# One layer of a diffusion backbone on one core: another order of the seven products of the FFNs' second matmul, later modulation vectors, and the final norm piece by piece

## The chip, the cores and the metric

The kernel runs on one core of a Trainium2 chip. The metric is the device time of one execution in microseconds; the median of the runs of one kernel is compared with the median of another's on the same chip.

## What is computed

One layer over 1024 latent tokens (width 1024) with 256 context tokens as a prefix: a half-step SwiGLU FFN, a mixer (short convolution beside attention, merged by gates), a second half-step FFN, and a final RMS norm. Each part is normed first and modulated by shift, scale and gate, nine vectors (`ml[0]` to `ml[8]`) that come from a small matmul of SiLU(c) with `w_mod`. Context tokens go through the first FFN and the mixer's projections only.

```python
def swiglu(h, w_in, w_out):
    a, b = jnp.split(h @ w_in, 2, axis=-1)
    return (jax.nn.silu(a) * b) @ w_out
...
        mod_lat = (jax.nn.silu(c) @ w_mod[layer] + b_mod[layer])[:, None, :]
...
        x = x + 0.5 * ml[2] * swiglu(modulate(rms_norm(x, norm1_g[layer]), ml[0], ml[1]),
                                      ffn1_w_in[layer], ffn1_w_out[layer])
...
        x = x + ml[5] * merge_branches(y_conv_l, o_l, gt_l, w_branch_conv[layer],
                                       w_branch_attn[layer], w_out[layer])
...
        x = x + 0.5 * ml[8] * swiglu(modulate(rms_norm(x, norm3_g[layer]), ml[6], ml[7]),
                                      ffn2_w_in[layer], ffn2_w_out[layer])
    return rms_norm(x, final_g)
```

## The kernel before

All matmuls are made of three: each 32-bit operand is split into a high part (a cast, on ACT) and a low part (a subtraction, on DVE), and high x high, high x low and low x high are added in PSUM. Left parts of weights are called `wl` and `wh` (two names, four buffers each, either holds both halves), right parts `rh`, `rl` or `r`.

Large products are taken as 2x2 blocks with seven block products instead of eight. The class `Winograd` does this for the products with columns of weights (the first matmul of both FFNs and the mixer), `row_products` for the FFNs' second matmul. There the right side is the hidden rows `hid` (22 rows of 128, upper and lower 11, left and right half: blocks b11, b12, b21, b22), written to DRAM as `hd` by the first matmul and fetched again. The left side is `w_out`, whose combinations are either loaded raw (products 1, 2, 4; two raw loads and a subtraction for product 7) or built in `ws` tiles by loads that add into them (`plus`, issued on GpSimd's queue; products 5, 6, 3). One product goes over 11 elements in 6 groups of two; each element is 12 matmuls, for 4 column tiles. Products 1, 6 and 7 add into one chain of four PSUM tiles (two of `pt`, one `po`, one `ps`), which is read out by adds into the latents `x` after each; the others use `ps` tiles. The hidden blocks are combined in place between products (`hid<-hid,hid` on DVE).

The stages, by time in the profiled execution: first FFN's first products until 720 us; its row products until 946, with the context's part of that FFN put in between in the last third of the first products; product 3's end and the norm that opens the mixer, until 972; the mixer until 1350; attention heads and merge until 2150; the second FFN's first products (the object `fast`) until about 2550; its row products until 2712; then product 3 of the second FFN, in two halves of 256 columns with its split operands held (`kept`), with the final norm beside it, until the end at 2768. In the second half `kept` is used again, one column tile after the other, each followed by its add into `x`.

The norm's scale for 512 columns comes as: squares (`sq`, ACT), sums by matmuls with a vector of ones into `pt`, an inverse square root on DVE (`rs_a`, `rs_y`), transposes with `ident` that spread it over partitions, and a multiplication of `x` by it, after which the shifted `x` is split into `r`. The final norm instead multiplies by a gain (`yf`), transposes `yf` into PSUM and scales the result on its way out (`ot`).

Modulation vectors 2 to 8 are made beside the first FFN's products: for each, `later_mod` loads rows of `w_mod` (`rawm`) and multiplies and adds them on DVE (`macc`), casts the sum on ACT (`acch`, `accl`), and finishes it with small matmuls, a copy and small stores and adds. It is a generator, of which a loop takes some steps a turn: `STEPS` in the first FFN, 11 in the mixer, and what is left at the mixer's end.

A scheduler places the instructions: each engine executes its list in order, and the order of the lists comes from a timeline made when the kernel is built, except for instructions that are pinned to program order. A step that waits therefore holds up everything behind it in its engine's list. SP's list issues most loads; its queue is a ring of eight.

The changed code in the kernel before:

Of the kernel before, what the change touches and what calls it, by code (L numbers as in the profile page):

```python
# [13 lines left out]
ALU = mybir.AluOpType  # L14
# [27 lines left out]
STEPS = (0, 6, 6, 6, 7, 7, 8, 8, 8, 15)  # L42
# [7 lines left out]
def tile_dit_layer(  # L50
# [413 lines left out]
    class Winograd:  # L464
# [6 lines left out]
        def __init__(self, xs, gain, mod, m, pairs, plain=False, ahead=3, side_from=None):  # L471
# [10 lines left out]
            self.n_squares = 0  # L482
# [18 lines left out]
        def norm0(self, in_place=False):  # L501

            acc = sum_squares(self.xs, C0)
            yield
            y = rstd_cols([acc], 512, D)
# [10 lines left out]
        def square(self, d):  # L516

            if not self.n_squares:
                self.acc = [ttile("sq_acc")]
            sq = ttile("sq") if self.n_squares else self.acc[0]  # L520
            act.activation(out=sq, in_=self.xs(d, C1), func=AF.Square)
            if self.n_squares == KD - 1:
                self.acc.append(sq)
            elif self.n_squares:
                dve.tensor_add(out=self.acc[0], in0=self.acc[0], in1=sq)
            self.n_squares += 1

        def norm1(self):
            y = rstd_cols(self.acc, 512, D)
# [215 lines left out]
    class Rows:  # L745


        def __init__(self, n, name):

            self.n, self.t = n, {}  # L750
# [15 lines left out]
        def fetch(self, src):  # L766

            for lower, c in ((0, 0), (0, 1), (1, 0), (1, 1)):
                for k, m in self.groups:
                    j = lower * self.n + k  # L770
                    load(self.t[k, lower, c], src[j : j + m, :, c * 512 : (c + 1) * 512].rearrange("a p n -> p a n"))

    def row_products(w, rows, add, after=lambda i, k: None, halves=False):
# [9 lines left out]

        R, groups = P * rows.n, rows.groups
        sums = {}
# [12 lines left out]

        def minus(t):
            act.activation(out=t, in_=t, func=AF.Copy, scale=-1.0)  # L800
# [13 lines left out]

        def operands(i, k, m):

            b11, b12, b21, b22 = (rows.t[k, v, c] for v in range(2) for c in range(2))
# [46 lines left out]
        for i in (1, 2, 4, 5, 6, 7) + (() if halves else (3,)):  # L864
            ps = chain if i in (1, 6, 7) else [ps_s() for _ in range(4)]
            for k, m in groups:
# [123 lines left out]
    half1.acc = accs  # L990
# [39 lines left out]
    def all_later_mods():  # L1030
# [5 lines left out]
        for m in range(2, 9):  # L1036
            yield from later_mod(m)

    steps = all_later_mods()


# [68 lines left out]

    gate1 = half_gate("gate1", 2)
# [22 lines left out]
    hs = Rows(NH // 2, "hid")  # L1134
    hs.fetch(hd)
# [570 lines left out]
```

## Time and profile before

| what | value |
|---|---|
| median of 3 runs | 2775.6 us (2775.3 to 2777.56) |
| profiled execution, own time | 2770.1 us |
| its span | 2768.2 us |
| granted TensorE clock, mean | 0.981 |
| PE (TensorE) busy | 96% |
| DVE (VectorE) busy | 73% |
| ACT (ScalarE) busy | 42% |
| POOL (GpSimd) busy | 20% |
| data moved | 354.37 MB, 128 GB/s on average |

A helper issues every instruction, so nearly all of them carry one line, 88, and the tile names tell them apart: `pt<-rh,wl` is a matmul into PSUM tile `pt` with those operands. A bracket at the end of a timeline's row gives how long the engine was idle before it and what ended that.

### The profile page before, as it was taken

What the parts mean: (1) busy time and instruction counts of PE and PEld (TensorE: products, weight loads), DVE (VectorE), ACT (ScalarE), POOL (GpSimd) and SP (SyncE); (2) the same over time, 40 slices, a digit from 0 to 9 for tenths busy, and PEclk for the clock granted to TensorE, in tenths of its full rate; (3) what the DMA queues carried; (4) which work ended last, traced back from release to release, by engine and by line L of the source; (5) the groups of instructions that cost most, each with busy time, mean ns of one, the idle gap of its engine ahead of it and who ended that gap; (6) DMA issues with size and microseconds to landing.
All of it is one profiled execution on the core that took longest, in us unless ns stands there. A gap on an engine that the chain in (4) does not pass through costs nothing.

```text
span 2768.2 us, 37334 instructions
## 1 busy us (share of the span) xinstructions
PE 2668.4 (96%) x13625; PEld 2248.5 (81%) x13625; DVE 2012.0 (73%) x3356; ACT 1153.5 (42%) x2293; POOL 543.0 (20%) x419
## 2 busy tenths in 40 slices
PE   7898999999799999999999999999999999999989
PEld 4687988888677777788899888887888788888878
DVE  5887688887787789887568676685548776568874
ACT  4524333333244552333344566574226333334542
POOL 2240122221011014333123211100000442330110
PEclk8899999999899999999999999999999999999999
DMA  8265433444965244434312311001444542228641
GB/s 308 92 203 159 137 122 122 135 131 150 369 188 112 92 152 151 157 99 134 107 47 63 117 62 61 24 32 41 150 125 129 168 130 76 85 91 292 147 98 62
DMA packets 355649, 354.37 MB, mean 128 GB/s; under 512 B 27382, under 2 KB 248712, under 8 KB 355464
## 3 DMA queue, kind: packets, MB, share of 16 engines
q1 hardware_dynamic: 346440, 334.68, 36.7%
q0 software_dynamic: 9024, 17.30, 4.0%
q8 instruction: 107, 1.75, 0.3%
q14 instruction: 78, 0.64, 0.1%
HBM read 287.91 MB, written 63.96 MB: 127 GB/s over the span
## 4 chain that ended last, share of the span: by engine, by line
PE 80%; DVE 10%; DMA 4%; issue 3%; ACT 2%; POOL 1%; SPq 1%; DVEq 0%; ACTq 0%; POOLq 0%
PE ps L88 66%; PE po L88 7%; PE pt L88 7%; DMA raw<-in_ffn_w_out_dram 2%; DVE wl L88 1%; DVE r L88 1%; DVE macc L88 1%; DMA rawm<-in_w_mod_dram 1%; DVE nt L88 1%; SPq L88 1%; DVE x L88 0%; DMA mcol<-mrow 0%; DVE hid L88 0%; DVE u L88 0%; DVE wo L88 0%
## 5 line engine op out<-in xcount | busy, mean ns | idle before, releaser
L88 PE MATMUL ps<-r,wl 128*128 128x512 f32 x5280 | 1234.2, 393 | 25.4 <-ACT r L88 9.8
L88 PEld LDWEIGHTS ps<-r,wl 128*128 128x128 f32 x5280 | 992.5, 189 | 242.3 <-ACT r L88 12.4
L88 ACT CAST wl<-s 128x512 fp32r<-128x512 f32 x256 | 158.3, 620 | 361.8 <-PE ps L88 270.6
L88 ACT CAST wl<-raw 128x512 fp32r<-128x512 f32 x278 | 172.0, 620 | 283.7 <-PE ps L88 173.5
L88 POOL TENSOR_TENSOR s<-raw 128x512 f32<-128x512 f32 x64 | 97.3, 1521 | 976.3 <-DMA raw<-in_ffn_w_in_dram 553.5
L88 DVE TENSOR_TENSOR wl<-raw,wl 128x512 fp32r<-128x512 f32 x276 | 196.6, 713 | 85.5 <-ACT wl L88 84.2
L88 DVE TENSOR_TENSOR wl<-s,wl 128x512 fp32r<-128x512 f32 x256 | 223.9, 876 | 13.4 <-ACT wl L88 11.7
L88 POOL TENSOR_TENSOR s<-raw,s 128x512 f32<-128x512 f32 x64 | 101.0, 1579 | 404.7 <-DVE wl L88 404.7
L88 DVE SCALAR_TENSOR_TENSOR macc<-rawm,silu_c,macc 128x512 f32<-128x512 f32 x168 | 146.6, 891 | 16.7 <-DMA rawm<-in_w_mod_dram 15.7
L88 PE MATMUL ps<-wh,r 128*128 128x256 f32 x768 | 141.6, 285 | 0.0
L88 DVE TENSOR_TENSOR u<-u,ps 128x512 f32<-128x512 f32 x168 | 114.4, 681 | 34.9 <-PE ps L88 33.3
L88 DVE TENSOR_TENSOR pts<-pt,pts 128x512 fp32r<-128x512 f32 x160 | 108.7, 687 | 42.1 <-ACT pts L88 41.0
L88 ACT CAST rh<-hid 128x512 fp32r<-128x512 f32 x132 | 80.7, 620 | 135.7 <-PE ps L88 103.5
L88 DVE TENSOR_REDUCE m<-ps 128x1 f32<-128x512 f32 (+1 forms) x192 | 110.9, 596 | 28.7 <-PE ps L88 27.7
L88 PE MATMUL ps<-rh,wl 128*128 128x512 f32 x360 | 126.1, 393 | 3.5 <-DVE x L88 3.5
L88 ACT CAST pts<-pt 128x512 fp32r<-128x512 f32 x160 | 93.0, 592 | 86.6 <-PE pt L88 84.9
L88 PEld LDWEIGHTS ps<-wh,r 128*128 128x128 f32 x768 | 120.6, 192 | 0.0
L88 DVE TENSOR_TENSOR rl<-hid,rh 128x512 fp32r<-128x512 f32 x132 | 89.9, 687 | 31.1 <-PE ps L88 29.6
L88 PE MATMUL po<-pts,vh 128*128 128x512 f32 x256 | 110.3, 437 | 1.5 <-ACT pts L88 1.5
L88 PE MATMUL ps<-wl,r 128*128 128x256 f32 x384 | 108.8, 283 | 0.0
L88 ACT CAST wh<-raw 128x512 fp32r<-128x512 f32 (+1 forms) x84 | 67.1, 803 | 95.2 <-PE ps L88 80.2
L88 PE MATMUL ps<-kl,qs 128*128 128x512 f32 x384 | 106.0, 397 | 0.4 <-ACT pc L88 0.4
(280 smaller groups left out, 5098.6 us busy)
## 6 DMA issues: line engine op xcount, KB each, us to landing
raw<-in_ffn_w_in_dram SPq DMA_DIRECT2D x117, 512.0 KB, 4.5
raw<-in_ffn_w_out_dram SPq DMA_DIRECT2D x72, 512.0 KB, 5.7
rawm<-in_w_mod_dram SPq DMA_DIRECT2D x128, 256.0 KB, 4.3
raw<-in_w_in_dram SPq DMA_DIRECT2D x61, 512.0 KB, 3.7
hid<-hd SPq DMA_DIRECT2D x40, 512.0 KB, 9.4
ws<-in_ffn_w_out_dram POOLq DMA_DIRECT2D x30, 512.0 KB, 6.5
hd<-c SPq DMA_DIRECT2D x38, 256.0 KB, 2.0
hd<-u SPq DMA_DIRECT2D x38, 256.0 KB
```

The costliest lines, as they stand in the source:

```text
L88: inst = getattr(self.engine, name)(*args, **kw)
```

## The change

1. The row products of both FFNs run as 2, 1, 4, 6, 5, 7, 3 instead of 1, 2, 4, 5, 6, 7, 3. The sums of hidden blocks are made differently, in `sums`, pinned, some groups behind the product that needs the old blocks; hidden rows are fetched by group as the products come to them (`fetches`), instead of all at once. The `ws` tiles begin in product 1's last groups and product 4 as `s1`, and a negated copy `s2` is made of each in product 4.
2. Modulation vectors 6, 7 and 8 leave the first FFN: 13 steps a turn in the mixer (before: 11 steps of what was left), 3 a turn in the second FFN's first products. `STEPS` ends in 12 instead of 15. Vectors 2 to 5 are complete before the first FFN's row products. `gate3`, which needs vector 8, moves behind the second FFN's first products.
3. The mixer's first norm: the squares of the columns C0 are taken as its columns are done, the scale is begun before product 3 and spread in its fourth group, and the halves are applied at groups 0 and 4.
4. The final norm of columns 0 to 511 is spread over products 5 and 3; the last 256 columns go through `last_final`, which sums and transposes each column tile as it comes and keeps four PSUM tiles to the end.

The diff, cut:

```diff
-STEPS = (0, 6, 6, 6, 7, 7, 8, 8, 8, 15)
+STEPS = (0, 6, 6, 6, 7, 7, 8, 8, 8, 12)
...
+        def fetches(i, g):
+            if i == 2:
+                rows.fetch(1, 0, g + 3)
+                rows.fetch(1, 1, g + 1)
+                rows.fetch(0, 0, g - 2)
+            elif i == 1:
+                rows.fetch(0, 0, g + 5)
+                rows.fetch(0, 1, g + 2)
+        def sums(i, g):
+            n = len(groups)
+            if i == 2 and g >= 2 or i == 1 and g < 2:
+                k, _ = groups[g - 2 if i == 2 else n - 2 + g]
+                _, _, b21, b22 = blocks(k)
+                dve.tensor_sub(out=b21, in0=b21, in1=b22)
+            if i == 1 and g or i == 4 and g == 0:
+                k, _ = groups[g - 1 if i == 1 else n - 1]
+                b11, b12, b21, _ = blocks(k)
+                dve.tensor_sub(out=b11, in0=b12, in1=b11)
+                dve.tensor_add(out=b21, in0=b21, in1=b11)
+            if i == 1 and g >= 3 or i == 4 and g < n - 3:
+                k, m = groups[g - 3 if i == 1 else n - 3 + g]
+                s1[k] = atile("ws", (P, 2, 512))[:, :m]
+                load(s1[k], block(k, m, 0, 1))
+                plus(s1[k], k, m, 1, 1)
+            k, m = groups[g]
+            b11, b12, _, b22 = blocks(k)
+            if i == 4:
+                dve.tensor_sub(out=b11, in0=b11, in1=b22)
+                s2[k] = atile("ws", (P, 2, 512))[:, :m]
+                act.activation(out=s2[k], in_=s1[k], func=AF.Copy, scale=-1.0)
+                plus(s2[k], k, m, 0, 0)
+            elif i == 6:
+                dve.tensor_add(out=b11, in0=b11, in1=b22)
+                plus(s2[k], k, m, 1, 0)
+            elif i == 5:
+                dve.tensor_sub(out=b12, in0=b22, in1=b12)
...
-                left = sums[k]
+                left = (s1 if i == 5 else s2)[k]
...
-            if i == 1:
-                dve.tensor_sub(out=b11, in0=b12, in1=b11)
-            elif i == 2:
-                dve.tensor_sub(out=b21, in0=b21, in1=b22)
-                dve.tensor_add(out=b21, in0=b21, in1=b11)
-            elif i == 4:
-                sums[k] = atile("ws", (P, 2, 512))[:, :m]
-                load(sums[k], block(k, m, 0, 1))
-                plus(sums[k], k, m, 1, 1)
-            elif i == 5:
-                minus(sums[k])
-                plus(sums[k], k, m, 0, 0)
-                dve.tensor_sub(out=b11, in0=b11, in1=b22)
-            elif i == 6:
-                plus(sums[k], k, m, 1, 0)
-                dve.tensor_sub(out=b12, in0=b22, in1=b12)
...
-        for i in (1, 2, 4, 5, 6, 7) + (() if halves else (3,)):
+        for i in (2, 1, 4, 6, 5, 7) + (() if halves else (3,)):
...
                 for e, lr in enumerate(operands(i, k, m)):
+                    if e == 0:
+                        fetches(i, g)
                     step(i, ps, k + e, *lr)
+                strict[0] = True
+                sums(i, g)
+                strict[0] = False
...
-        for m in range(2, 9):
+        for m in range(2, 6):
             yield from later_mod(m)
-    steps = all_later_mods()
+    steps, late_steps = all_later_mods(), (step for m in (6, 7, 8) for step in later_mod(m))
...
+    run(steps)
     gate1 = half_gate("gate1", 2)
...
-    hs.fetch(hd)
+    hs.fetch(1, 0, 2)
...
-    residual = {(1, 4): (C0, 0), (2, 2): (C0, 4), (2, 8): (C1, 0), (4, 4): (C1, 4)}
+    residual = {(2, 4): (C0, 0), (1, 6): (C0, 4), (4, 8): (C1, 0), (6, 4): (C1, 4)}
...
-                if ch == C1:
-                    mix.square(d)
+                mix.square(d, ch)
...
-            if i == 2:
+            if i == 1:
                 done(range(4), C0)
             elif i == 7:
                 done(range(4, KD), C0)
+                run(norms2, 1)
                 done(range(4, KD), C1)
...
-        if i == 3 and k in (0, 2, 4, 6):
+        if i == 3 and k in (0, 4):
             run(norms2, 1)
...
         if i > 1:
-            run(steps, 11)
+            run(late_steps, 13)
...
-    run(steps)
...
-    last_chunks = (C0, ("l", 512, 256), ("l", 768, 256))
-    finals = [final(ch) for ch in last_chunks]
+    def last_final(ch):
...
+        def turn(k, y):
+            for j in js:
+                if k % 4 == 0:
+                    pts[j, k // 4] = ps_s()
+                transpose(pts[j, k // 4][:, k % 4 * P : (k % 4 + 1) * P], y[:, j * P : (j + 1) * P], pinned=True)
+        def add_up(sq, start, stop):
+            for j in js:
+                matmul(
+                    sums[:, j : j + 1], sq[:, j * P : (j + 1) * P], ones[:], start=start and j == 0, stop=stop,
+                    pinned=True, on=j > 0,
+                )
...
+        for k in range(4):
+            sq, y = ready(k)
+            if k < 3:
+                turn(k, y)
+            add_up(sq, False, k == 3)
+            if k < 3:
+                yield
+        turn(3, y)
...
+    finals = [final(C0, range(KD)), final(("l", 512, 256), (4, 5, 6, 7, 0, 1, 2, 3)), last_final(("l", 768, 256))]
     fast.start(fast.norm1())
     for j in range(NH):
+        if j > 1:
+            run(late_steps, 3)
...
-        if i == 8 and k == 8:
-            run(finals[0], 4)
+        if i == 5 and k in (2, 4, 6, 8):
+            run(finals[0], 1)
+        if i == 8 and k < 10:
+            run(finals[0], 1)
+        if (i, k) == (8, NH // 2):
+            run(finals[1], 4)
         if i == 9:
             run(finals[0], 1)
-            if k >= 2:
-                run(finals[1], 1)
-            if k in (9, 10):
-                run(finals[2], 2)
+            run(finals[1], 1)
+            if 2 < k < 11:
+                run(finals[2], 1)
```

How this moves the instructions, at three places. First, ACT's list where the first FFN's first products end and its row products begin. Before (`u` and `c` belong to the last hidden rows, `sa` and `hidc` to the context, `rh` is the first right part of the row products):

```order
L88 CAST hidc_6363<-sa_6571 128x256
L88 COPY mrow_6615<-pt_6612 1x512
L88 ACTIVATE u_6434<-u_6434 128x512
L88 CAST wh_6819<-raw_6798 128x512
L88 CAST wh_6860<-raw_6839 128x512
L88 CAST wl_6882<-raw_6880 128x512
L88 CAST wh_6901<-raw_6880 128x512
L88 CAST wl_6931<-raw_6929 128x512
L88 CAST wh_6950<-raw_6929 128x512
L88 CAST acch_6648<-macc_1133_6623 128x512
L88 CAST rh_6803<-hid_6748 128x512
L88 CAST rh_6822<-hid_6748 128x512
```

Now:

```order
L88 CAST wl_6673<-raw_6671 128x512
L88 ACTIVATE sa_6502<-po_6364 128x256
L88 CAST wl_6719<-raw_6717 128x512
L88 CAST hidc_6298<-sa_6502 128x256
L88 CAST rh_6676<-hid_6641 128x512
L88 CAST rh_6701<-hid_6641 128x512
L88 CAST wl_6762<-raw_6760 128x512
L88 ACTIVATE u_6365<-u_6365 128x512
L88 CAST wh_6698<-raw_6671 128x512
L88 CAST wh_6741<-raw_6717 128x512
L88 CAST rh_6722<-hid_6645 128x512
```

The cast of a modulation vector is gone from ahead of `rh`, and two `rh` stand ahead of the last hidden row's activation. The third right part's low half stands on DVE behind the context's multiply-adds now:

```order
L88 TENSOR_TENSOR wh_6783<-raw_6760,wh_6783 128x512
L88 SCALAR_TENSOR_TENSOR cx_6619<-cacc_1012,gate_c,cx_6619 128x256 x2
L88 SCALAR_TENSOR_TENSOR cx_6624<-cacc_1012,gate_c,cx_6624 128x256 x2
L88 SCALAR_TENSOR_TENSOR cx_6629<-cacc_1013,gate_c,cx_6629 128x256 x2
L88 SCALAR_TENSOR_TENSOR cx_6634<-cacc_1013,gate_c,cx_6634 128x256 x2
L88 TENSOR_TENSOR rl_6723<-hid_6645,rh_6722 128x512
```

Two such rows of one operation are written as one with x2. Second, PE's list at the end of the first FFN's product 3. Before (`wh_8555` is the last of its eleven elements, `rs_y` the scale of the mixer's norm, `r` the mixer's right side):

```order
L88 MATMUL ps_8281<-wh_8555,wl_8552 128x512 x3
L88 MATMUL ps_8282<-wh_8555,wl_8552 128x512 x3
L88 MATMUL ps_8283<-wh_8555,wl_8552 128x512
L88 MATMUL pt_8435<-ident,rs_y_8387 128x128 x4
L88 MATMUL ps_8283<-wh_8555,wl_8552 128x512 x2
L88 MATMUL ps_8284<-wh_8555,wl_8552 128x512 x3
L88 MATMUL ps_8606<-r_1471_8442,wl_8591 128x512 x3
```

Now (`wh_8461` is the last element, `wh_8407` the eighth):

```order
L88 MATMUL ps_8231<-wh_8407,wl_8404 128x512 x3
L88 MATMUL pt_8269<-ident,rs_y_8202 128x128 x4
L88 MATMUL ps_8232<-wh_8407,wl_8404 128x512 x3
L88 MATMUL ps_8229<-wh_8425,wl_8422 128x512 x3
L88 MATMUL ps_8230<-wh_8425,wl_8422 128x512 x3
L88 MATMUL ps_8231<-wh_8425,wl_8422 128x512 x3
L88 MATMUL ps_8232<-wh_8425,wl_8422 128x512 x3
L88 MATMUL ps_8229<-wh_8443,wl_8440 128x512 x3
```

The scale's transposes stand 39 matmuls ahead of the first `r` (the rows shown, and the last two elements), where 5 stood. Third, PE's list at the program's end: before, 8 transposes (`ident,yf`) of the middle 256 columns, 12 sums (`ones,sq`) and 16 transposes of the last 256 followed the last `kept` matmul; the first rows of these:

```order
L88 MATMUL ps_24643<-kept_24389,kept_24386 128x256 x3
L88 MATMUL ps_24739<-ident,yf_24581 128x128 x2
L88 MATMUL ps_24739<-ident,yf_24634 128x128 x2
L88 MATMUL po_24745<-ident,yf_24450 128x128 x2
L88 MATMUL po_24745<-ident,yf_24519 128x128 x2
L88 MATMUL pt_24766<-ones,sq_24660 128x1
```

Now the list ends so:

```order
L88 MATMUL ps_24754<-ident,yf_24613 128x128
L88 MATMUL ps_24756<-ident,yf_24613 128x128
L88 MATMUL pt_24739<-ones,sq_24793 128x1 x2
L88 MATMUL ps_24767<-kept_24356,kept_24353 128x256 x3
L88 MATMUL ps_24767<-kept_24374,kept_24371 128x256 x3
L88 MATMUL ps_24767<-kept_24396,kept_24393 128x256 x3
L88 MATMUL ps_24767<-kept_24414,kept_24411 128x256 x3
L88 MATMUL ps_24767<-kept_24463,kept_24460 128x256 x3
L88 MATMUL pt_24739<-ones,sq_24816 128x1 x2
L88 MATMUL ps_24754<-ident,yf_24613 128x128
L88 MATMUL ps_24756<-ident,yf_24613 128x128
```

Two sums and two transposes are left behind the last `kept` matmul; the others of the last 256 columns stand between the column tiles. Over the whole program DVE has 12 more instructions (3368 for 3356), PE two more.

More of the change, by code (lines that the diff above doesn't have):

```diff
@@ L813, in parts, with blocks @@
             return t
+        def blocks(k):
+            return (rows.t[k, v, c] for v in range(2) for c in range(2))
+        def fetches(i, g):
[34 more added lines that the diff above has]
+                dve.tensor_sub(out=b12, in0=b22, in1=b12)
         def operands(i, k, m):
-            b11, b12, b21, b22 = (rows.t[k, v, c] for v in range(2) for c in range(2))
+            b11, b12, b21, b22 = blocks(k)
             if i in (1, 2, 4):
@@ L1623, in final, with scaled_out, ready @@
             yield
-    last_chunks = (C0, ("l", 512, 256), ("l", 768, 256))
-    finals = [final(ch) for ch in last_chunks]
+    def scaled_out(ot, pt, half, scale):
+        oh = ot[:, half * 512 : (half + 1) * 512]
+        if half:
+            act.activation(out=oh, in_=pt, func=AF.Copy, scale=scale)
+        else:
+            dve.tensor_scalar(out=oh, in0=pt, scalar1=scale, scalar2=None, op0=ALU.mult)
+    def last_final(ch):
+        s, o, n = ch
+        js = range(n // P)
+        y2 = [atile("yf", (P, 4, 256)) for _ in range(2)]
+        pts, sums = {}, None
+        def ready(k):
+            sq, y = ttile("sq", n), y2[k // 4][:, k % 4]
+            act.activation(out=sq, in_=xs(k, ch), func=AF.Square)
+            dve.tensor_scalar(out=y, in0=xs(k, ch), scalar1=gf[:, k : k + 1], scalar2=None, op0=ALU.mult)
+            return sq, y
+        def turn(k, y):
[8 more added lines that the diff above has]
+                    pinned=True, on=j > 0,
+                )
+        first = []
+        for k in (4, 5, 6, 7):
+            sq, y = ready(k)
+            if first:
+                dve.tensor_add(out=first[0], in0=first[0], in1=sq)
+            else:
+                first.append(sq)
+            yield
+        for k in (4, 5, 6, 7):
+            turn(k, y2[1][:, k % 4])
+        sums = ps_t(len(js))
+        add_up(first[0], True, False)
+        yield
+        for k in range(4):
+            sq, y = ready(k)
+            if k < 3:
+                turn(k, y)
+            add_up(sq, False, k == 3)
+            if k < 3:
+                yield
+        turn(3, y)
+        a = small("rs_a", len(js))
+        dve.tensor_scalar(out=a[:], in0=sums, scalar1=D * EPS, scalar2=None, op0=ALU.add)
+        rstd = rsqrt_cols(a[:], len(js))
+        for j in js:
+            ot = atile("ot")
+            for half in range(2):
+                scaled_out(ot, pts[j, half], half, rstd[:, j : j + 1])
+            sp.dma_start(out=out[0, o + j * P : o + (j + 1) * P, :], in_=ot[:])
+        yield
@@ L1633, in tile_dit_layer @@
         spill(*fast.third(u, v), j, C1)
-    hs = Rows(NH // 2, "hid")
-    hs.fetch(hd)
+    run(late_steps)
+    gate3 = half_gate("gate3", 8)
+    hs = Rows(hd, NH // 2, "hid")
+    hs.fetch(1, 0, 2)
     def add3(d, ch, t):
```

71 lines of the change are left out of this document (33 added, 38 removed).

## The prediction

> **What bounds the kernel now.** I read the page's head first, then busy time by stretches, because the head is an average.
>
> ```profile
> span 2768.2 us, 37334 instructions
> PE 2668.4 (96%) x13625; PEld 2248.5 (81%) x13625; DVE 2012.0 (73%) x3356; ACT 1153.5 (42%) x2293; POOL 543.0 (20%) x419
> ```
>
> TensorE is busy 96% of the span and the change leaves its matmuls as they are, so all that can move is what it waits for. The stretches (PE, PEld, DVE, ACT, POOL busy, then granted clock, DMA share, GB/s) say where that is:
>
> ```profile
> 330.00:720.00 390.00, 385.33 (x2153) 334.71 (x2152) 314.78 (x485) 132.60 (x240) 77.96 (x49) 1.00 0.47 151
> 720.00:736.00 16.00, 0.43 (x1) 0.43 (x2) 9.10 (x15) 2.75 (x6) 0.00 (x0) 0.61 1.01 355
> 736.00:798.00 62.00, 62.00 (x263) 50.71 (x263) 56.71 (x79) 25.62 (x46) 7.17 (x6) 0.96 0.93 289
> 798.00:946.00 148.00, 143.24 (x625) 117.83 (x624) 103.87 (x154) 67.51 (x117) 14.07 (x12) 0.99 0.47 114
> 946.00:972.00 26.00, 19.29 (x77) 15.14 (x76) 18.50 (x39) 14.48 (x24) 0.00 (x0) 0.80 0.25 81
> 972.00:1350.00 378.00, 373.00 (x1640) 305.05 (x1640) 319.20 (x483) 137.48 (x240) 122.68 (x80) 1.00 0.42 134
> 2200.00:2250.00 50.00, 50.00 (x222) 41.40 (x222) 39.74 (x50) 16.14 (x27) 21.57 (x14) 1.00 0.52 167
> 2550.00:2650.00 100.00, 99.08 (x437) 81.55 (x436) 77.65 (x112) 48.68 (x85) 17.69 (x15) 1.00 0.70 157
> 2650.00:2690.00 40.00, 33.07 (x141) 26.67 (x140) 34.41 (x53) 19.15 (x36) 3.39 (x3) 0.91 0.50 115
> ```
>
> The undisturbed pace is 50.00/222 = 0.225 us for a matmul 512 wide; in second FFN first products DVE is busy 39.74 us of 50 and PE loses nothing, so DVE only matters where it gates a tile. By that pace 720 to 736 loses nearly all its 16 us, 736 to 798 loses 62.0 - 263 x 0.225 = 2.8 (the clock is at 0.96 after the gap), 798 to 946 loses 7.3, 946 to 972 some 9.7 (69 of its 77 are such matmuls, 15.5 us; the other 8 take 0.8), 972 to 1350 about 8.7, 2550 to 2690 loses 140 - 578 x 0.225 = 9.9. Those are the places that the change touches.
>
> **Transition to the row products (720 to 736).** The timeline there:
>
> ```profile
> 684.59 0.33 SPq L88 DMA_DIRECT2D hd<-c  x1
> ...
> 722.48 4.67 SPq L88 DMA_DIRECT2D rawm<-in_w_mod_dram  x7
> 728.87 5.48 DVE L88 SCALAR_TENSOR_TENSOR macc<-rawm,silu_c,macc 128x512 f32<-128x512 f32 x7 [5.18 <-DMA rawm<-in_w_mod_dram]
> 734.38 0.62 ACT L88 CAST acch<-macc 128x512 fp32r<-128x512 f32 x1 [11.50 <-DVE macc L88]
> 734.91 1.66 ACT L88 CAST rh<-hid 128x512 fp32r<-128x512 f32 x3
> 735.57 1.22 PE L88 MATMUL pt<-rh,wl 128*128 128x512 f32 x2 [15.92 <-ACT rh L88]
> ```
>
> PE waits 15.92 us for the first right part; ACT would cast it, but a modulation vector's cast, `acch`, stands ahead in its queue and waits 11.50 us for seven multiply-adds on DVE, which wait for their loads. The change takes those vectors away and casts product 2's first right parts before the last hidden row exists. What can go is 15.9 + 2.8 of slow clock = 18.7. Late next: right parts from the second group on. On DVE eight context multiply-adds of 128x256 stand ahead of `rl_6723` (8 x 0.47 by the tail's row below = 3.8 us); their loads stand on SP's queue behind 14 `hid`, 2 `raw` and 8 `x` loads, with themselves 11.5 MB, at the 355 GB/s shown 32 us. The store `hd<-c` ahead of them goes at 684.6, and 1.5 MB issued just before it takes 4.2 more: 689, so they land at about 721; PE has 24 matmuls, 5.4 us, in hand, until 725; 721 + 3.8 + one subtraction of 0.68 is 725.5, and a landing as slow as those of `rawm` (5.18 waited) would make it later. I take a stall of 2.2 there: **-16.5** (-11 with a stall of 7.5, -18.7 with none).
>
> **FFN1's row products.** DVE subtractions and additions between hidden blocks become 12 more per kernel; a 128x1024 one takes 2.49/2 = 1.25 us:
>
> ```profile
> 736.96 2.49 DVE L88 TENSOR_TENSOR hid<-hid,hid 128x1024 f32<-128x1024 f32 x2
> ```
>
> That is 15 us more on DVE, over both FFNs, beside 226 + 162 us of matmuls with DVE at 170 and 118 busy: hidden; uncovered, it would cost at most 7.5 in each. Products 1, 6, 7 add into one set of PSUM tiles. Before, 7 followed 6 directly, so its first matmul waited for the reads of 6; now 5 stands between, and 4 between 1 and 6. SP's and POOL's queues carry the same loads, later and by group. Of the 7.3 lost I take **-4.8** (0 to -7): DVE's load is highest in product 1, which now holds most sums.
>
> **Start of the mixer (946 to 972).**
>
> ```profile
> 954.63 0.60 PE L88 MATMUL pt<-ident,rs_y 128*128 128x128 f32 x4
> 955.85 4.87 DVE L88 TENSOR_TENSOR x<-x,pt 128x512 f32<-128x512 f32 x8
> 959.80 0.79 PE L88 MATMUL ps<-r,wl 128*128 128x512 f32 x1 [3.41 <-ACT r L88]
> 963.89 8.54 PE L88 MATMUL ps<-r,wl 128*128 128x512 f32 x25 [3.30 <-DVE r L88]
> ```
>
> The transposed scale comes with 5 matmuls of product 3 left, and the first `r` is used 959.80 - 954.63 = 5.2 us later, the second set 9.3 later. Now 39 matmuls, 8.8 us, follow the transposes: the first wait is covered, the second almost. Against it: product 3's four adds and squares fall into the same queues. I leave 3 of the 9.7: **-6.7** (-2 to -9).
>
> **Modulation vectors moved.** 24 multiply-adds leave the transition, the mixer gets 10 more (34 for 24), the second FFN's first products 14.
>
> ```profile
> L88 DVE SCALAR_TENSOR_TENSOR macc<-rawm,silu_c,macc x112: 736/745/1781, 346.1 to 696.1; 128x512 f32<-128x512 f32 x112
> 1116.14 4.24 DVE L88 SCALAR_TENSOR_TENSOR macc<-rawm,silu_c,macc 128x512 f32<-128x512 f32 x3
> PE ps L88 <- DVE wl L88: 4.0, 4, 3.0
> ```
>
> 10 x 0.745 = 7.5 us against 378 - 319 = 59 idle on DVE: 0 by cover. Without cover it is a burst as at 1116, after which one wait of PE for a left part is 3.0. Mixer **0** (-3 to +6), second FFN's first products **+0.5** (0 to +6, two bursts); on SP their loads pass between weight loads. FFN1 itself loses 390 - 385.3 = 4.7 now and gets 12 steps instead of 15 a turn: **-1.5** (-4 to +1).
>
> A rule that speaks against this: the Trainium skill, SBUF — State Buffer, "SBUF: two separate sides", calls the port pair shared by VectorE and GpSimd an exclusive lock, so that a VectorE operation with two SBUF inputs is blocked for a whole GpSimd instruction that reads SBUF. The longest `macc`, 1781 for 745 ns, agrees; that rule makes the sum 24.9 worse if each moved one were blocked and seen.
>
> **FFN2's row products.**
>
> ```profile
> 2664.57 0.62 ACT L88 CAST kept<-ws 128x512 fp32r<-128x512 f32 x1 [5.67 <-DMA ws<-in_ffn_w_out_dram]
> 2681.74 0.77 PE L88 MATMUL pt<-rh,wl 128*128 128x512 f32 x1 [4.31 <-DVE x L88]
> ws<-in_ffn_w_out_dram POOLq DMA_DIRECT2D x30, 512.0 KB, 6.5
> ```
>
> ACT waits 5.67 us for an accumulating load in front of casts that product 6 needs, and PE 4.31 for the adds between 6 and 7. Both go: 5's and 4's casts stand there instead, and 5 lies between. Of 9.9 and some 1.7 of the same kind around it I take **-9.5** (-3 to -11). Late next may be the negation `s2<-s1`, pinned on ACT, which waits for a load of that kind.
>
> **Product 3 in halves and the final norm.**
>
> ```profile
> 2690.00:2712.00 22.00, 22.00 (x99) 18.22 (x98) 6.29 (x10) 4.57 (x8) 0.00 (x0) 1.00 0.05 14
> 2717.75 16.60 PE L88 MATMUL ps<-kept,kept 128*128 128x256 f32 x137
> 2721.51 0.68 DVE L88 TENSOR_TENSOR kept<-ws,kept 128x512 fp32r<-128x512 f32 x1
> 2756.35 0.47 DVE L88 SCALAR_TENSOR_TENSOR x<-ps,gate_l,x 128x256 f32<-128x256 f32 x1
> 2756.98 2.74 PE L88 MATMUL pt<-ones,sq 128*128 128x1 f32 x24
> 2759.75 0.16 DVE L88 TENSOR_SCALAR rs_a<-pt 128x2 f32<-128x2 f32 x1 [1.21 <-PE pt L88]
> 2761.97 0.69 ACT L88 ACTIVATE ot<-po,rs_y 128x512 f32<-128x512 f32 x1 [4.06 <-DVE rs_y L88]
> 2762.72 0.66 PE L88 MATMUL po<-ident,yf 128*128 128x128 f32 x4 [1.63 <-ACT ot L88]
> 2763.41 0.69 ACT L88 ACTIVATE ot<-po,rs_y 128x512 f32<-128x512 f32 x1 [0.75 <-PE po L88]
> ...
> 2763.15 1.30 SPq L88 DMA_DIRECT2D out_dram<-ot  x2
> ```
>
> Before, DVE idles through product 7's end (6.29 busy of 22), most kept parts being made. Now only two elements are; the third's stand behind product 7's eight adds and a piece of the final norm: 8 x 0.68 + 0.4 + 2 x 0.68 = 7.2 us after product 7. PE has 24 x 0.121 = 2.9 us of the two elements (0.121 is 16.60/137), and pieces of the next column, some 4.5 in all: **+3** (+1 to +4.5).
>
> Tail: after the last product's last matmul (2756.2), sums, scale, transposes and the second `ot`, which waited for a PSUM bank, take to the span's end, 12.0 us. Now transposes come with the column tiles, and there remain the add of 0.47, a square, two sums, the scale (2759.75 to 2761.97, 2.2), two `ot` and the last store (issued near 2764.1, so 4.1 to the span's end): some 9.4, a gain of 2.6. But the 3.8 us of sums and transposes do not vanish: they are done between the tiles, ahead of that last matmul, and four PSUM tiles are held to the end, so that a tile's product can wait for a bank: +0.8. Net **+2** (0 to +4).
>
> **Sum.** -16.5 - 4.8 - 6.7 + 0 + 0.5 - 1.5 - 9.5 + 3 + 2 = -33.5. I add one new wait of PE of the mixer's size, 3.0, for a place that I did not see: **-30.5**. The profiled execution took 2770.1 us (span 2768.2), so 2739.6; the median of the runs is 2775.6, 5.5 above, so **2745**. The runs differ by 2.3 us, 0.08%; 0.2% (5.6 us) is about what can be told from no change.
>
> **Rivals.**
> *Waits given back.* The moved vectors gate left parts in the mixer (3.0 each, as at 1116) in three or four places, +10; the context loads cost the 7.5 at the transition, +5; kept parts +1.5 more, tail +2. For it: every one of those queues is nearly as full as before. Against: the DVE idle time above. -30.5 + 18.5 = -12: 2763.6 (2754 to 2770).
> *The lock.* With 24 moved multiply-adds each blocked by 1781 - 745 = 1.04 us, 24.9 us, all seen by PE, it would be -5.6; half of them, -18: 2758. Against: POOL is busy 123 of 378 us in the mixer, so a third would be hit.
> *Slower: the negation.* Six per FFN of `s2<-s1` stand pinned on ACT, each after a load that may take 5.67 us to wait for, and all casts of right parts queue behind them. If each of 12 shows fully, 68 us: +37, 2813. It decides from 30.5/12 = 2.5 us each. Against: the load is issued three groups, 3 x 5.4 us, before, and takes 6.5.
> *No change.* The stall at 720 is of DMA: share 1.01, 355 GB/s. If the hidden rows' loads simply end as late, the transition keeps its 16 us, and the other gains fall to half with it, -5.
>
> **Chances.** Forecast (-22 to -46) 0.71; given back 0.14; lock 0.03; no change 0.07; slower 0.05. Faster by over 0.2%: 0.71 + 0.14 + 0.03 = 0.88; within: 0.07; slower: 0.05. The range goes from 2775.6 - 44.6 = 2731 (the gains near their ends together) to 2762 in the middle of the second case, which leaves out half of that, no change and slower, and a tail of 0.02 below: 0.2.
>
> **What would show it.** Right: at the end of FFN1 PE goes on within 3 us; no wait over 2 at the mixer's start; PE busy over 158 us of the 162 of FFN2's row products; a new wait of 1 to 4 for `kept` after product 7; 9 to 10 us from the last kept matmul to the end. Wrong: waits for `wl` in the mixer, for `rl` behind `cx`, or ACT waiting for `ws` before `s2`.

## The result and the profile after

The changed kernel takes 2739.01 us (median of four runs, 2735.13 to 2741.85) against 2775.8 before: the ratio is 0.9865, with a 95% interval of 0.9848 to 0.9882. The forecast was 2745 (2731 to 2762). The profiled execution took 2737.3 us, 32.8 less than the one before.

The head of the page after, and busy time by stretches (us, then PE, PEld, DVE, ACT, POOL busy, granted clock, DMA share, GB/s). The stages end earlier now: the first FFN's first products at 715, its row products and product 3 at 936, the mixer at 1334, the second FFN's products 1 to 7 at 2674:

```profile
span 2735.6 us, 37415 instructions
PE 2662.7 (97%) x13629; PEld 2246.2 (82%) x13629; DVE 2021.2 (74%) x3368; ACT 1152.3 (42%) x2293; POOL 547.9 (20%) x419
```

```profile
330.00:715.00 385.00, 384.66 (x2154) 335.02 (x2153) 301.60 (x466) 131.75 (x238) 81.12 (x49) 1.00 0.44 141
715.00:777.00 62.00, 60.67 (x268) 49.60 (x267) 54.63 (x79) 25.83 (x46) 5.03 (x4) 1.00 0.93 296
777.00:904.00 127.00, 122.66 (x529) 100.34 (x530) 95.27 (x137) 56.32 (x97) 16.22 (x14) 0.99 0.60 145
904.00:936.00 32.00, 32.00 (x152) 26.76 (x152) 27.10 (x54) 20.38 (x35) 0.00 (x0) 1.00 0.16 63
936.00:950.00 14.00, 14.00 (x72) 11.89 (x71) 11.86 (x21) 9.34 (x18) 0.00 (x0) 1.00 0.58 186
950.00:1334.00 384.00, 376.65 (x1644) 308.19 (x1643) 328.67 (x496) 140.22 (x242) 124.51 (x80) 0.99 0.45 142
2495.00:2674.00 179.00, 179.00 (x791) 148.26 (x791) 144.63 (x206) 79.55 (x139) 21.09 (x18) 1.00 0.66 171
2674.00:2726.00 52.00, 50.90 (x401) 49.86 (x399) 34.00 (x86) 20.20 (x42) 0.00 (x0) 0.93 0.15 62
```

PE is busy all of 179 us in the second FFN's products, all of the 46 from 904 to 950 where the norm stood, and over the first transition. What is left in the changed stages lies in 715 to 904, in the mixer and in the last stage. The timeline at three places (start, length, engine, operation, and in brackets the idle time before and what ended it) shows the gap at the transition closed, the scale's transposes followed by 39 matmuls and then the first `r` with no wait, and a new wait between products 1 and 4:

```profile
709.56 5.92 PE L88 MATMUL ps<-hidc,wo 128*128 128x256 f32 x48
715.32 0.40 PE L88 MATMUL ps<-rh,wl 128*128 128x512 f32 x1
...
926.76 0.60 PE L88 MATMUL pt<-ident,rs_y 128*128 128x128 f32 x4
927.12 9.11 PE L88 MATMUL ps<-wh,wl 128*128 128x512 f32 x39
936.07 4.24 PE L88 MATMUL ps<-r,wl 128*128 128x512 f32 x18
...
776.69 1.66 ACT L88 ACTIVATE sq<-x 128x512 f32<-128x512 f32 x3
778.26 1.12 ACT L88 CAST rh<-hid 128x512 fp32r<-128x512 f32 x2
778.92 1.20 PE L88 MATMUL ps<-rh,wl 128*128 128x512 f32 x4 [2.84 <-ACT rh L88]
```

To compare stages I add up, over all matmuls, how much longer the time from one's start to the next's is than the usual one of that width (0.227 us for 512 columns), and call it time lost. It holds both waits and matmuls at a lower clock: of the 18.6 at the transition, 16.1 is the wait and 2.5 the slow matmuls behind it. Three runs out of the experiments stand beside it (the last two are the changed kernel with that one piece put back); the first 300 us, which no kernel changes, differ by up to 1.9 between runs, so smaller differences tell nothing.

| us lost by PE | before | after | vectors moved alone | old first norm | old final norm |
|---|---|---|---|---|---|
| first FFN's first products | 7.7 | 2.9 | 3.7 | 2.8 | 2.8 |
| transition | 18.6 | 0 | 0 | 0 | 0 |
| first FFN's row products | 7.0 | 8.7 | 7.4 | 6.7 | 8.8 |
| product 3's end, mixer's start | 10.2 | 0 | 9.9 | 9.5 | 0 |
| mixer | 9.0 | 12.5 | 9.5 | 9.6 | 13.9 |
| second FFN's products 1 to 7 | 11.0 | 0 | 9.7 | 0 | 17.5 |
| its product 3 (kept) | 1.5 | 4.6 | 1.5 | 4.6 | 1.4 |
| last kept matmul to the span's end (length) | 12.3 | 10.2 | 12.0 | 10.2 | 12.1 |

### The profile page after: what moved, and what is told of

Same layout as the page of the kernel before. It is cut to its first block, busy times and chain, and to the rows that moved or that the text cites. A ratio compares the mean times of both kernels' runs of the same rounds, so it can differ in the third digit from the quotient of the medians.

```text
span 2735.6 us, 37415 instructions
## 1 busy us (share of the span) xinstructions
PE 2662.7 (97%) x13629; PEld 2246.2 (82%) x13629; DVE 2021.2 (74%) x3368; ACT 1152.3 (42%) x2293; POOL 547.9 (20%) x419
## 4 chain that ended last, share of the span: by engine, by line
PE 55%; DVE 4%; ACT 1%; issue 1%; DMA 1%; POOL 0%; DVEq 0%; SPq 0%; POOLq 0%; ACTq 0%
PE ps L88 46%; PE pt L88 5%; PE po L88 4%; DVE wl L88 1%; DVE y L88 0%; DVE macc L88 0%; DVE u L88 0%; DVE ol L88 0%; ACT pts L88 0%; DVE v L88 0%; DVE r L88 0%; POOL s L88 0%; DVE x L88 0%; DVE pts L88 0%; DMA rawm<-in_w_mod_dram 0%
```

## The experiments

Two theories stood against each other on the largest term. M: the gap at the transition is the modulation vector's cast on ACT. D: it is the transfer of all hidden rows at once. Each edit below is to the changed kernel unless it says otherwise.

**Vectors put back.**

```diff
-STEPS = (0, 6, 6, 6, 7, 7, 8, 8, 8, 12)
+STEPS = (0, 6, 6, 6, 7, 7, 8, 8, 8, 15)
-        for m in range(2, 6):
+        for m in range(2, 9):
...
-            run(late_steps, 13)
+            run(steps, 11)
```

> The changed kernel with modulation vectors 6 to 8 put back where they were (15 steps a turn in the first FFN, 11 in the mixer, the rest at its end); order, fetches, first norm and final norm as changed. Theory M (the gap of 16 us at the first FFN's row products is the vector's cast ahead of the first right part): the gap is back, 14 to 19 us lost near 720, 2755 to 2760 us, some 17 to 21 above the changed kernel. Theory D (the gap is the transfer of all hidden rows at once, which fetching by group removes): no gap over 4 us there, 2736 to 2744.

2759.05 us (2756.49 to 2761.73), ratio to before 0.9946 (0.9931 to 0.9961). The timeline of this run at the transition has the gap back, in spite of the new order and the fetches by group:

```profile
730.54 5.48 DVE L88 SCALAR_TENSOR_TENSOR macc<-rawm,silu_c,macc 128x512 f32<-128x512 f32 x7 [5.87 <-DMA rawm<-in_w_mod_dram]
736.05 0.62 ACT L88 CAST acch<-macc 128x512 fp32r<-128x512 f32 x1 [12.18 <-DVE macc L88]
...
737.24 2.07 PE L88 MATMUL ps<-rh,wl 128*128 128x512 f32 x4 [16.64 <-ACT rh L88]
```

M holds. The vectors' place also sets what the first products before lose: 7.7 again.

**Vectors moved alone**, in the kernel before (the same edit the other way).

> The kernel before with the move of modulation vectors 6 to 8 alone. Theory M: the gap at 720 is gone, first FFN 4 shorter as in the changed kernel, the mixer 3 longer: 2775.8 - 18.6 - 4 + 3 = 2756 (2752 to 2761). Theory D: the gap stays at 8 to 16 us since 24 loads of hidden rows are still issued at once: 2764 to 2775.

2747.75 us (2747.25 to 2749.9), ratio 0.9907 (0.9892 to 0.9921): M again, and more than expected: by the ratios this part alone brings some 26 of the 37 us. I had charged it with 3 us in the mixer, which lost 9.5 (9.0 before). The row products lose 7.4 for 7.0, so closing the gap cost them next to nothing in sum. But a wait that was not there before stands in the row products, behind a late load:

```profile
759.08 0.62 ACT L88 CAST wl<-raw 128x512 fp32r<-128x512 f32 x1 [1.35 <-DMA raw<-in_ffn_w_out_dram]
759.75 0.80 PE L88 MATMUL ps<-rh,wl 128*128 128x512 f32 x1 [2.68 <-ACT wl L88]
```

The gap of 16 us had given the loads time.

**Row products as before** (order, sums of blocks and fetches), with everything else changed.

```diff
-        for i in (2, 1, 4, 6, 5, 7) + (() if halves else (3,)):
+        for i in (1, 2, 4, 5, 6, 7) + (() if halves else (3,)):
...
-    hs.fetch(1, 0, 2)
+    hs.fetch(hd)
```

> The changed kernel with the row products as before in both FFNs (order 1, 2, 4, 5, 6, 7, 3, all hidden rows fetched at once, sums as before); vectors, first norm and final norm as changed. Theory M: the order is worth the second FFN's row products alone, 11 us lost there again, and 0 to 2 less lost in the first FFN's: 2739 + 10 = 2749 (2745 to 2753). Theory D: the transition's gap is back too: 2757 to 2768.

2747.93 us (2743.35 to 2749.24), ratio 0.9903 (0.9888 to 0.9918). The total is the one expected, its parts are not: the first FFN's row products lose 14.5 (8.7 with the new order), the second FFN's only 2.6 (not 11). PE's waits in the first FFN's row products of this run (us in total, times, longest):

```profile
PE ps L88 <- ACT wl L88: 3.5, 1, 3.5
PE ps L88 <- ACT rh L88: 2.8, 1, 2.8
PE pt L88 <- DVE x L88: 2.8, 1, 2.8
```

The first and the last stand in the run with the vectors moved alone too (2.7 and 2.8). The second does not, and product 4 loses 4.7 with it: ACT takes the squares of the new first norm ahead of product 4's right parts. So with the new first norm the order is worth 5.8 in the first FFN, and most of the 11 in the second went by something else.

**All hidden rows fetched at once**, in the new order.

```diff
-    hs.fetch(1, 0, 2)
+    for lower, c in ((1, 0), (1, 1), (0, 0), (0, 1)):
+        hs.fetch(lower, c, 6)
```

> The changed kernel, but all 24 loads of hidden rows are issued at the start of the row products in the order in which the products come to them, in place of by group. Theory M: 2739 + 0 to 4 (later raw loads queue behind them). Theory D: 8 or more us lost between 715 and 760, 2747 or more.

2757.78 us (2754.68 to 2761.93), ratio 0.9938 (0.9921 to 0.9954): here M's number is wrong and D's right. The first FFN's row products lose 19.6, the second's 12.4. PE goes on at 714 as it should, and stops after six elements of product 2, at a left part whose raw load stands behind the hidden rows' on SP's queue:

```profile
739.99 0.62 ACT L88 CAST wl<-raw 128x512 fp32r<-128x512 f32 x1 [3.22 <-DMA raw<-in_ffn_w_out_dram]
...
740.66 0.79 PE L88 MATMUL ps<-rh,wl 128*128 128x512 f32 x1 [10.36 <-ACT wl L88]
```

So both theories hold a part: the old gap was the vector's cast, and behind it lay a second limit, the loads, which the new order meets (with the cast gone) unless rows are fetched by group.

**First norm as before.**

```diff
-                mix.square(d, ch)
+                if ch == C1:
+                    mix.square(d, ch)
...
-                run(norms2, 1)
...
-        if i == 3 and k in (0, 4):
+        if i == 3 and k in (0, 2, 4, 6):
```

> The changed kernel with the mixer's first norm as before (squares of columns C0 taken in product 3, scale then, halves applied at groups 0, 2, 4, 6). Theory S (the early squares cost 3.0 us of PE at the start of product 4, and the early scale saves 10 at the mixer's start): some 10 us lost again at the mixer's start, the wait of 3.0 for a right part in front of product 4 gone: 7 above the changed kernel, 2743 to 2749. Rival N (the wait in front of product 4 is the order's own, with or without squares): the 3.0 stays, 9 to 11 above, 2748 to 2752.

2739.0 us (2736.96 to 2740.67), the changed kernel's own time. Neither expectation held. The 9.5 at the mixer's start are back and the wait of 3.0 between products 1 and 4 is gone, as S said; but 2.9 less is lost in the mixer (9.6 for 12.5), so that the profile is only 2.1 us longer and the median shows nothing: the new first norm by itself brought no time that these runs show. With the 3.0 gone, a wait of 4.3 stands at product 4's last element instead of smaller ones behind it. The first FFN's row products lose 6.7 here, against 7.4 with the old order and the old first norm (vectors moved alone): without the early squares the order is worth only 0.7 there, less than these sums can tell.

**Final norm as before.**

```diff
-    finals = [final(C0, range(KD)), final(("l", 512, 256), (4, 5, 6, 7, 0, 1, 2, 3)), last_final(("l", 768, 256))]
+    finals = [final(ch) for ch in last_chunks]
...
-        if i == 5 and k in (2, 4, 6, 8):
-            run(finals[0], 1)
```

> The changed kernel with the final norm as before. Theory O (the order takes the waits out of the second FFN's row products): they lose 0 to 2 us as in the changed kernel; product 3 in halves loses 1.5 for 4.6 and the tail is 12.3 for 10.2: within 3 us of the changed kernel. Rival F (the place of the kept casts and of the final norm's pieces took most of the 11 us, since with the old order and the new final norm only 2.6 were lost): 6 to 9 us lost there again, 2744 to 2749.

2750.93 us (2747.36 to 2752.84), ratio 0.9917 (0.9901 to 0.9934). Rival F, and by more than it gave: the second FFN's products lose 17.5 us with the new order in place. The timeline there:

```profile
2590.49 2.16 POOL L88 DMA_DIRECT2D ws<-in_ffn_w_out_dram  x2 [6.78 <-issue]
2596.77 1.21 POOL L88 DMA_DIRECT2D ws<-in_ffn_w_out_dram  x1 [4.11 <-issue]
2603.41 0.62 ACT L88 CAST kept<-ws 128x512 fp32r<-128x512 f32 x1 [21.68 <-DMA ws<-in_ffn_w_out_dram]
...
2603.93 0.61 ACT L88 CAST rh<-hid 128x512 fp32r<-128x512 f32 x1
...
2604.60 0.79 PE L88 MATMUL pt<-rh,wl 128*128 128x512 f32 x1 [13.63 <-ACT rh L88]
```

The wait is at product 6's third element, not at its first. One `kept` cast, for product 3, stands ahead of that element's right part and waits 21.68 us for the last of the loads that add into its `ws` tile. Where the scheduler puts that cast depends on what else there is to do later, and the final norm's pieces are that.

**The kept parts pinned**, with the old final norm.

```diff
+            strict[0] = where == "kept"
             split(src, *t)
+            strict[0] = False
```

> The changed kernel with the final norm as before (as the run with the final norm put back), and with the casts and subtractions of the kept parts of product 3 pinned to program order, so that all of them stand behind product 7's right parts on ACT. Theory K (the 13.8 us at the first matmul of product 6 is one kept cast on ACT that waits 21.7 us for an accumulating load, in front of the right part's cast): the second FFN's row products lose 0 to 2 in place of 17.5, the kept phase 2 to 6 more than 1.4: 2736 to 2742. Rival (the loads themselves are too late for product 6): 10 or more stay, 2746 or more.

2738.32 us (2735.39 to 2740.14), ratio 0.9865 (0.9851 to 0.988): the casts now stand behind product 7's right parts, the 17.5 are 0, the kept phase loses 9.6 for 1.4. That confirms K, with a larger price: net 12.6 us less. The old final norm with the casts pinned is as fast as the new one.

**The kept parts pinned in the kernel before.**

> The kernel before with the kept parts pinned in the same way and nothing else. Theory K: of the 11.0 us lost in the second FFN's row products 3 to 7 stay (the adds between products 6 and 7), the kept phase loses 2 to 6 more: 2769 to 2775. Theory O (only the order removes these waits): the 11 stay, and the total rises by the kept phase's loss: 2776 to 2780.

2774.33 us (2769.38 to 2779.7), ratio 1.0001 (0.9992 to 1.001). The second FFN's products lose 5.9 for 11.0, as K said; its product 3 loses 8.8 for 1.5, more than the 2 to 6 that K gave. The waits of this run of PE, from 2520 on (us in total, times, longest):

```profile
PE pt L88 <- DVE x L88: 3.8, 1, 3.8
PE ps L88 <- DVE x L88: 3.1, 2, 2.9
```

The first are the adds between products 6 and 7, which only the order takes away; the second are the adds after product 7, now ahead of the kept subtractions. So in the kernel before, early kept casts cost as much as they saved.

**Squares later.**

```diff
-                mix.square(d, ch)
+                if (i, ch) != (1, C0):
+                    mix.square(d, ch)
...
+        if i == 4 and k in (2, 4, 6, 8):
+            mix.square(k // 2 - 1, C0)
```

> The changed kernel, but the four squares of the first columns of C0 are taken one by one at groups 2, 4, 6 and 8 of product 4 and not all at the end of product 1. Theory S: the wait of 3.0 us in front of product 4 falls to under 0.5, 2 to 3 below the changed kernel. Rival N: it stays, since the reads of product 1's PSUM tiles hold the right parts up anyway; no change.

2736.57 us (2733.54 to 2738.86), ratio 0.9866 (0.9851 to 0.9881). The profile is 2.4 us shorter, which the runs can't tell from the changed kernel. The wait of 3.0 is gone (S), but the two waits that begin near 811 and 823 (1.0 and 1.4 lost) became one of 3.9, at product 4's last element, behind the pinned negation:

```profile
804.77 0.63 ACT L88 ACTIVATE ws<-ws 128x512 f32<-128x512 f32 x1 [9.00 <-DMA ws<-in_ffn_w_out_dram]
...
807.28 0.58 PE L88 MATMUL ps<-rl,wl 128*128 128x512 f32 x1 [3.94 <-DVE rl L88]
```

**Late vectors spread.**

```diff
-            run(late_steps, 13)
+            run(late_steps, 8)
...
                 run(merge(j, ch))
+                run(late_steps, 2)
```

> The changed kernel with 8 steps of the late vectors a turn in the mixer in place of 13, and two after each merge, so that vectors 6 and 7 are ready as late as the second FFN needs them. Theory B (the wait of 3.3 near 1089 and a part of 0.9 near 1139 are bursts of six to seven multiply-adds on DVE that hold up the read of a PSUM tile or a left part): the mixer loses 8 to 9.5 in place of 12.5, the merge no more than 1 more; 2 to 4 below the changed kernel. Rival: any burst of four does it, and the wait only moves to another turn: no change.

2732.54 us (2729.92 to 2741.87), ratio 0.9858 (0.9837 to 0.9879): the interval overlaps the changed kernel's, but the profile is 7.5 us shorter and shows where. The mixer loses 7.6 for 12.5, the merge 0.4 more: theory B, and better than it said (1.2 of the 7.5 stand in the first 300 us, which no kernel changes). In the changed kernel the wait that goes looked like this:

```profile
1082.80 5.60 DVE L88 SCALAR_TENSOR_TENSOR macc<-rawm,silu_c,macc 128x512 f32<-128x512 f32 x6 [0.65 <-DMA rawm<-in_w_mod_dram]
1088.43 0.62 ACT L88 CAST acch<-macc 128x512 fp32r<-128x512 f32 x1 [8.56 <-DVE macc L88]
...
1092.77 2.82 PE L88 MATMUL ps<-r,wl 128*128 128x512 f32 x7 [3.18 <-ACT wl L88]
```

It is the old gap's mechanism in small: a burst of multiply-adds on DVE, ACT's list standing at the vector's cast, and behind that the cast that PE needs. The waits of PE in the mixer, of the changed kernel and of this run:

```profile
PE ps L88 <- DVE wl L88: 3.7, 2, 3.0
PE ps L88 <- ACT wl L88: 3.5, 2, 3.2
```

```profile
PE ps L88 <- DVE wl L88: 3.2, 2, 2.8
PE ps L88 <- ACT wl L88: 1.1, 2, 0.9
```

**Both (the last two edits together), and then with the sums begun earlier.**

> The changed kernel with the squares taken later and the late vectors spread, both. Theory: 2739 - 2.4 - 6.5 = 2730 (2727 to 2734), with the wait of some 4 us near the third element of the first FFN's product 6 for the accumulating load as with the squares alone.

2731.29 us (2727.38 to 2733.57), ratio 0.984 (0.9825 to 0.9854), as expected, with a wait of 4.7 behind the negation (at product 4's last element, as with the squares alone, not in product 6).

```diff
-            if i == 1 and g >= 3 or i == 4 and g < n - 3:
-                k, m = groups[g - 3 if i == 1 else n - 3 + g]
+            if i == 1 and g >= 2 or i == 4 and g < n - 4:
+                k, m = groups[g - 2 if i == 1 else n - 2 + g]
```

> The same, and in addition the tiles s1 begin one group earlier (product 1 from its third group, product 4 in its first two). Theory G (ACT's pinned negation waits up to 9.7 us for the accumulating load that was issued three groups earlier): that wait goes, the first FFN's row products lose 2 to 4 less: 2724 to 2730. Rival (GpSimd's queue issues the load no earlier, since it waits its turn there): no change against the run without it.

2726.35 us (2724.64 to 2728.55), ratio 0.9821 (0.9805 to 0.9838) to before, some 13 below the changed kernel: the fastest version, and its interval lies clear of the changed kernel's. G holds: PE no longer waits behind the negation, and the row products lose 5.1 for 7.0, with a new wait of 2.8 in product 1. That is 1.9 of the 4.9 us between the two medians; 1.7 more stand in the mixer, at a wait that both runs have, behind which only the other run's clock fell (see the last section). PE's waits from 700 to 1340 in this run:

```profile
PE ps L88 <- DVE wl L88: 3.4, 2, 3.0
PE pt L88 <- DVE wl L88: 2.8, 1, 2.8
PE ps L88 <- DVE rl L88: 0.5, 1, 0.5
```

## Why the prediction was right, term by term

| term | predicted | measured | what the runs showed |
|---|---|---|---|
| transition | -16.5 | -18.6 | the vector's cast, as said; the context loads did not stall it |
| first FFN's row products | -4.8 | +1.7 | wrong sign: the old waits went, the squares and the negation brought new ones |
| mixer's start | -6.7 | -10.2 | the second wait is covered too |
| mixer | 0 | +3.5 | the new first norm and the moved vectors together |
| second FFN's first products | +0.5 | 0 | cover holds |
| first FFN's first products | -1.5 | -4.8 | two waits at 534 and 592 went with the vectors |
| second FFN's products | -9.5 | -11.3 | size right, cause half wrong (from 11.0 lost to 0.3 under the usual pace) |
| kept | +3 | +3.1 | right by luck: the wait for `kept` that was forecast is 0.3; waits in all are some 1 us, the rest a lower clock |
| tail | +2 | +2.3 | 2.1 shorter at the end, 4.4 of work moved ahead (products 1 to 7 and kept took 234.4 us with 12.5 lost, now 230.6 with 4.3 lost) |
| a place not seen | +3.0 | 0 | nothing left over for it: the new waits stand in the rows above |

The transition carried the forecast, and the runs with the vectors put back and moved alone show it. The measured terms add up to -34.3; the span fell by 32.6, with 1.5 more lost in the first 300 us, that no kernel changes, and 0.7 less in the merge, which leaves 0.9 unaccounted for. That the sum lies so near is in part luck: misses of +6.5 in the first FFN's row products and +3.5 in the mixer met misses of -3.5, -3.3, -2.1 and -1.8 elsewhere and the 3.0 held in reserve. Two steps failed.

The step "Of the 7.3 lost I take **-4.8**" failed. The base was right: with the gap gone and everything else in these products as before they lose 7.4 (vectors moved alone). The waits that were to go did go: product 7's first matmul no longer waits for the reads of 6. But I counted the early squares with the mixer only: four of them stand on ACT ahead of product 4's right parts, and product 4 loses 4.9 for that, 3.0 as a wait, which moving the squares removed. And the negation, which the sum put at nothing, costs as much wherever the early squares do not: 3.9 to 4.7 waited at product 4's last element in the runs without them, until the sums began a group earlier. So in the first FFN the order is worth 0.7 with the old first norm (7.4 to 6.7) and 5.8 with the new one (14.5 to 8.7), and order and new norm together made it worse, 7.0 to 8.7.

The step "Both go: 5's and 4's casts stand there instead, and 5 lies between" was right about the adds (3.8 of them stay with the old order when casts are pinned) and wrong about the kept casts: they moved because of the final norm's pieces, not because of the order. With the old final norm the order alone makes it worse, 17.5. I took a side effect of the scheduler for a property of the order.

The rivals. "Waits given back" happened in part: mixer +3.5, kept +3.1, tail +2.3, the squares 3.0; it did not reach 18.5. "No change" took the gap for the loads': the runs with the vectors put back and moved alone decide against it, and the run with all rows fetched at once shows what was right in it. "Slower: the negation" exists: ACT waited 9.7 us for the load in front of it in the changed kernel, so the three groups were too short a lead, but PE lost only some 2 us there (and waited 3.9 to 4.7 once an earlier wait was gone), in the first FFN alone. Of the three signs of being wrong, two came: waits for `wl` in the mixer, and ACT waiting for `ws` before the negation.

"The lock": the multiply-adds in the mixer had a median of 747 ns and went up to 1777. Seven of the 29 took over 1 us; each of these began while a TENSOR_TENSOR of GpSimd was running, and none of the other 22 did. Together the seven took 5.3 us more than the median, some 0.8 us each. The Trainium skill, SBUF — State Buffer, "SBUF: two separate sides", says that of a VectorE operation with two SBUF inputs and a GpSimd operation that reads SBUF, whichever starts first has the shared ports for the whole instruction, and the other is blocked. The trace agrees in these seven. No run here shows a cost of it on PE by itself: with the late vectors spread such operations were still there, up to 1779 ns, and the mixer's loss went all the same, which points at the bursts. The changed kernel's multiply-adds in the mixer (count, then shortest, median and longest in ns), and ACT's wait for the loads ahead of the negation in the first FFN's row products (us in total, times, longest):

```profile
L88 DVE SCALAR_TENSOR_TENSOR macc<-rawm,silu_c,macc x29: 740/747/1777, 1079.6 to 1305.7; 128x512 f32<-128x512 f32 x29
```

```profile
ACT ws L88 <- DMA ws<-in_ffn_w_out_dram: 13.0, 2, 9.7
```

Left open: the wait of 3.0 us for `wl` some 55 us into the mixer (lost there: 1.9 with the old first norm and the vectors moved, 3.0 to 4.3 in every run with the new one). Right parts of the norm stand ahead of that `wl` on DVE, but no run was made for it. Open too is why the clock fell in the kept phase, where PE had no long wait.

## What to carry to other kernels

A gap in the bound engine hides what else is late: after it is closed, the loads or the casts behind it show, so read the stages after a gap as if they started with no slack. An instruction that is not urgent but waits for a load (a cast for a later product) may stand ahead of urgent ones in an in-order list; pin it behind them, and look in the changed kernel where it now stands, since any other work can move it. Parts of a change are not additive: every piece here moved some wait to another place, and only the runs that undid one at a time told which had paid (the vectors and the order did; the new first norm did not, and the final norm only by where it left the kept casts).

## What was not expected of the hardware

Loads that add into a tile, 512 KB each, went out from GpSimd's queue one or two at a time, 6 to 7 us apart (2590.49, 2596.77, 2603.63 in the run with the old final norm), with a median of 6.5 us from issue to landing in the kernel before; the profile does not show what held them. So a lead of three groups, counted against one transfer of 6.5 us, was too short: ACT waited up to 9.7 us for the load ahead of the negation, and with a lead of four groups that wait was gone.

The price of a wait of PE depends on the granted clock behind it. Behind the wait of 2.8 us ahead of product 4 in the changed kernel the granted clock was 0.57 from 779.5 to 783.5, and matmuls came up to 0.43 us apart in place of 0.227, so that product 4 lost 4.9. With the late vectors spread, the same wait of 2.8 was followed by a clock of 1.00 (777.5 to 781.5), and product 4 lost 3.3. So some 1.6 us at one and the same wait come and go with the clock. In the kept phase the clock was 0.50 from 2698.5 to 2701.7 and from 2708.7 to 2711.9, and before the change in one such stretch (2737.6 to 2740.8): at some 1.5 us each, that is the slower pace of the kept term.
